# Linear attention with relu features on one core: four heads per 128 partitions for K and V, masked K, and nine output stores queued behind the loads

## The chip, the core and the metric

The kernel runs on one core of a Trainium2 chip. The metric is device time in microseconds (us). Before the change it is 131.75 us, the median of 10 runs that lie between 131.35 and 132.35 us.

## What is computed

The inputs Q, K and V and the output are float32 tensors of shape (8, 12, 512, 64): batch, heads, sequence, head dimension. Cut to what matters:

```python
Q_feat = np.maximum(0, Q)
K_feat = np.maximum(0, K)
KV = einsum('bhkd,bhkv->bhdv', K_feat, V)        # per head: 64 x 64
K_sum = sum(K_feat, axis=2)                      # per head: 64
numerator = einsum('bhqd,bhdv->bhqv', Q_feat, KV)
denominator = einsum('bhqd,bhd->bhq', Q_feat, K_sum)
out = numerator / (denominator[..., None] + 1e-10)
```

There are 96 heads in all, each independent of the others. A head's K, V, Q and output are 128 KB each in float32, so the core has to read 37.75 MB and write 12.58 MB.

## The kernel before

**Tiling.** The 96 heads are cut into 24 groups of four (NG = 24). One group's Q is a tile of 128 partitions by 1024 values: a head takes 32 partitions, and each partition holds 16 consecutive sequence rows of 64, which are 4 KB of consecutive DRAM in float32. The output has the same layout. K and V have another layout: two pairs of heads, and in each pair a head takes 64 partitions with 8 sequence rows each. A partition therefore reads two separate runs of 2 KB (`rview`, with j the pair).

**Loads.** All loads but the first K and V cast float32 to bfloat16 on the way and are issued from GpSimd (POOL): `load_kv` (L81 for K, L83 for V) and `load_q` (L87). They stand in one queue, q0 in the profile, in program order. Every DMA of that queue waits for the one eight places ahead of it, so at most eight are in flight. K and V of group 0 come in float32 over SP and ACT (L91, L93). K and V have 20 buffers each; Q has one for every group.

**Stores.** Group g's output leaves as 512 KB in float32 (`store`). Groups 0 to 16 and 22 leave over SP (L189, queue q1). Group 23 leaves over SP in two halves (L186). The five groups 17 to 21 (HELD = 5) leave over POOL (L182). All loads are issued ahead of them in POOL's program, so these stores stand behind every load in q0.

**Steps of one group.** The order is written out by hand in the last loop:

- `prep(g)` on VectorE (DVE): relu of K into bfloat16, written twice side by side (L114, 128x2048), and two copies of V into the halves of a block-diagonal tile `vbd` with a column of ones per head (L120, 64x1024 each). The zeros of `vbd` are written once for each of its three buffers (`zero`, L105 to L108).
- `mm_kv(g)` on TensorE (PE): for each of two pairs and eight rows r one matmul, 128 rows deep, 128 columns of K as weights and 130 columns of `vbd` moving (L128), 16 in all. Because `vbd` is block-diagonal, the two heads of a pair stay apart.
- `evac_kv(g)` on ScalarE (ACT): two copies of the sums from PSUM into a block-diagonal tile `kvd` (L137, 64x260).
- `transp(g)` on PE: eight 128x128 transposes of Q (L143), and `evac_qt(g)` on ACT: relu from PSUM to SBUF (L147).
- `mm_out(g)` on PE: 32 matmuls with 32 weight columns and 130 moving ones (L158), and `norm(g)` on DVE: denominator, reciprocal and product for two halves (L169, L171, L172), then the store.

The loop runs `mm_kv(g)`, `evac_kv(g)`, `prep(g+1)`, then `mm_out(g-1)` with `norm(g-1)` and its store, then `transp(g)` and `evac_qt(g)`. Each engine takes its instructions in that order. The sums of `mm_kv` have two PSUM buffers.

Of the kernel before, what the change touches and what calls it, by code (L numbers as in the profile page):

```python
# [9 lines left out]
@with_exitstack  # L10
def kernel(
    ctx: ExitStack,
    tc: tile.TileContext,
    Q: bass.AP,
    K: bass.AP,
    V: bass.AP,
    out: bass.AP,
):
    nc = tc.nc
    B, H, S, D = Q.shape  # L20
    assert D == 64
    P = 128
    D1 = D + 1
    NH = B * H


    R = S * 2 // P
    RQ = S * 4 // P
    PR = 2
    NHG = 2 * PR  # L30
    U = RQ // 2
    NG = NH // NHG
    assert NG * NHG == NH and R == 8 and RQ == 16
    HELD = 5

    fp32 = mybir.dt.float32
    bf16 = mybir.dt.bfloat16
    Act = mybir.ActivationFunctionType
    Alu = mybir.AluOpType

    def pool(name, bufs, **kw):
        return ctx.enter_context(tc.tile_pool(name=name, bufs=bufs, **kw))

    consts = pool("consts", 1)
    qin = pool("qin", NG)
    kin = pool("kin", 20)
    vin = pool("vin", 20)
    kfp = pool("kfp", 3)
    qtp = pool("qtp", 3)
    rcp = pool("rcp", 4)  # L50
    outp = pool("outp", 10)
    pkv = pool("pkv", 2, space=bass.MemoryType.PSUM)
    pqt = pool("pqt", 2, space=bass.MemoryType.PSUM)
    pou = pool("pou", 2, space=bass.MemoryType.PSUM)

    def rview(X):
        return X.rearrange("b h s d -> (b h s d)").rearrange(
            "(n j p f) -> n p j f", p=P, f=R * D, j=PR)

    def qview(X):  # L60
        return X.rearrange("b h s d -> (b h s d)").rearrange("(n p f) -> n p f", p=P, f=RQ * D)

    Qr, Kr, Vr, Or = qview(Q), rview(K), rview(V), qview(out)

    ident = consts.tile([P, P], bf16, name="ident")
    NB = 3

    vbf = [consts.tile([P, PR * R * 2 * D1], bf16, name=f"vbd{i}") for i in range(NB)]  # L70
    kvf = [consts.tile([P, PR * 2 * 2 * D1], bf16, name=f"kvd{i}") for i in range(NB)]
    vbd = [x.rearrange("p (j r h d) -> p j r h d", j=PR, r=R, h=2) for x in vbf]
    kvd = [x.rearrange("p (j h t d) -> p j h t d", j=PR, h=2, t=2) for x in kvf]

    ctx.enter_context(tc.manual_schedule())

    q_sb, k_sb, v_sb = {}, {}, {}

    def load_kv(g):
        k_sb[g] = kin.tile([P, PR, R, D], bf16, name="k_sb")  # L80
        nc.gpsimd.dma_start(out=k_sb[g].rearrange("p j r d -> p j (r d)"), in_=Kr[g])  # L81
        v_sb[g] = vin.tile([P, PR, R, D], bf16, name="v_sb")
        nc.gpsimd.dma_start(out=v_sb[g].rearrange("p j r d -> p j (r d)"), in_=Vr[g])  # L83

    def load_q(g):
        q_sb[g] = qin.tile([P, U, 2 * D], bf16, name="q_sb")
        nc.gpsimd.dma_start(out=q_sb[g].rearrange("p u f -> p (u f)"), in_=Qr[g])  # L87


    k_sb[0] = outp.tile([P, PR, R, D], fp32, name="k_first", tag="o_sb")  # L90
    nc.sync.dma_start(out=k_sb[0].rearrange("p j r d -> p j (r d)"), in_=Kr[0])  # L91
    v_sb[0] = outp.tile([P, PR, R, D], fp32, name="v_first", tag="o_sb")
    nc.scalar.dma_start(out=v_sb[0].rearrange("p j r d -> p j (r d)"), in_=Vr[0])  # L93
    load_q(0)
    make_identity(nc, ident)
    for g in range(1, NG - 2):
        load_kv(g)
        load_q(g)
    load_kv(NG - 2)
    load_kv(NG - 1)  # L100
    load_q(NG - 2)
    load_q(NG - 1)

    def zero(i):
        nc.vector.memset(vbf[i].bitcast(fp32), 0.0)  # L105
        for h in range(2):
            nc.vector.memset(vbd[i][64 * h:64 * h + 64, :, :, h, D:D1].rearrange("p j r o -> p (j r) o"), 1.0)
        nc.vector.memset(kvf[i].bitcast(fp32), 0.0)  # L108

    kf, qt, ps_kv, ps_qt, ps_out = {}, {}, {}, {}, {}  # L110

    def prep(g):
        kf[g] = kfp.tile([P, PR, R, 2, D], bf16, name="kf")
        nc.vector.tensor_scalar(  # L114
            kf[g].rearrange("p j r c d -> p (j r) c d"),
            k_sb[g].rearrange("p j r d -> p (j r) d").unsqueeze(2).to_broadcast([P, PR * R, 2, D]),
            scalar1=0.0, scalar2=None, op0=Alu.max)
        for h in range(2):
            hs = slice(64 * h, 64 * h + 64)
            nc.vector.tensor_copy(  # L120
                vbd[g % NB][hs, :, :, h, 0:D].rearrange("p j r d -> p (j r) d"),
                v_sb[g][hs].rearrange("p j r d -> p (j r) d"))

    def mm_kv(g):
        ps_kv[g] = pkv.tile([P, PR, 2, D1], fp32, name="ps_kv")
        for j in range(PR):
            for r in range(R):
                nc.tensor.matmul(  # L128
                    ps_kv[g][:, j, :, :],
                    kf[g][:, j, r, :, :].rearrange("p c d -> p (c d)"),  # L130
                    vbd[g % NB][:, j, r, :, :],
                    start=(r == 0), stop=(r == R - 1), skip_group_check=True)

    def evac_kv(g):
        for t in range(2):
            ts_ = slice(64 * t, 64 * t + 64)
            nc.scalar.copy(kvd[g % NB][ts_, :, :, t, :].rearrange("p j h d -> p (j h) d"),  # L137
                           ps_kv[g][ts_].rearrange("p j h d -> p (j h) d"))

    def transp(g):  # L140
        ps_qt[g] = pqt.tile([P, U, P], bf16, name="ps_qt")
        for u in range(U):
            nc.tensor.transpose(ps_qt[g][:, u, :], q_sb[g][:, u, :], ident)  # L143

    def evac_qt(g):
        qt[g] = qtp.tile([P, U, P], bf16, name="qt")
        nc.scalar.activation(  # L147
            qt[g].rearrange("p u q -> p (u q)"), ps_qt[g].rearrange("p u q -> p (u q)"), Act.Relu)

    def mm_out(g):  # L150
        for j in range(2):
            po = pou.tile([P, 2, 512], fp32, name="ps_out")
            ps_out[g, j] = po
            for v in range(U // 2):
                u = j * (U // 2) + v
                for h in range(NHG):
                    hs = slice(32 * h, 32 * h + 32)
                    nc.tensor.matmul(  # L158
                        po[hs, v // 2, (v % 2) * 2 * D1:(v % 2) * 2 * D1 + 2 * D1],
                        qt[g][:, u, hs],  # L160
                        kvd[g % NB][:, h // 2, h % 2, :, :],
                        start=True, stop=True, skip_group_check=True)

    def norm(g):
        o_sb = outp.tile([P, RQ, D], fp32, name="o_sb", tag="o_sb")
        for j in range(2):
            pv = ps_out[g, j][:, :, 0:4 * D1].rearrange("p b (r d) -> p b r d", d=D1)
            den = rcp.tile([P, 2, 4], fp32, name="den")
            nc.vector.tensor_scalar(den, pv[:, :, :, D], scalar1=1e-10, scalar2=None, op0=Alu.add)  # L169
            rec = rcp.tile([P, 2, 4], fp32, name="rec")  # L170
            nc.vector.reciprocal(rec, den)  # L171
            nc.vector.tensor_tensor(  # L172
                o_sb[:, 8 * j:8 * j + 8].rearrange("p (b r) d -> p b r d", b=2),
                pv[:, :, :, 0:D],
                rec.unsqueeze(3).to_broadcast([P, 2, 4, D]), op=Alu.mult)
        return o_sb

    def store(g, o_sb):  # L180
        if NG - 2 - HELD <= g < NG - 2:
            nc.gpsimd.dma_start(out=Or[g], in_=o_sb.rearrange("p r d -> p (r d)"))  # L182
        elif g == NG - 1:
            for j in range(2):
                rs = slice(RQ // 2 * j, RQ // 2 * (j + 1))
                nc.sync.dma_start(out=Or[g].rearrange("p (r d) -> p r d", d=D)[:, rs],  # L186
                                  in_=o_sb[:, rs])
        else:
            nc.sync.dma_start(out=Or[g], in_=o_sb.rearrange("p r d -> p (r d)"))  # L189

    zero(0)
    prep(0)
    for g in range(NG):
        mm_kv(g)
        evac_kv(g)
        if g + 1 < NG:
            if g + 1 < NB:
                zero(g + 1)
            prep(g + 1)
        if g > 0:  # L200
            mm_out(g - 1)
            store(g - 1, norm(g - 1))
        transp(g)
        evac_qt(g)
    mm_out(NG - 1)
    store(NG - 1, norm(NG - 1))


# [28 lines left out]
```

## Time and profile before

| what | value |
|---|---|
| median of 10 runs | 131.75 us (131.35 to 132.35) |
| the profiled execution's own time | 132.17 us |
| its span, first to last instruction | 130.4 us |
| PE busy | 78.0 us (60%), 1344 matmuls |
| weight loads (PEld) busy | 64.2 us (49%) |
| DVE busy | 90.2 us (69%) |
| ACT busy | 43.9 us (34%) |
| POOL busy | 51.9 us (40%) |
| granted TensorE clock, mean | 0.78 of full |
| DMA packets | 20126, 32.18 MB as written |
| read from and written to HBM | 37.75 MB and 12.58 MB, 386 GB/s over the span |

The span is the time from the first to the last instruction of the program; the profiled execution took 1.8 us more than its span. A casting load is counted by the bytes that it writes to SBUF, half of what it reads from DRAM: that is why the packets sum to 32.18 MB and the HBM traffic to 50.33 MB. The profile's "DMA share" is the summed time of all packets over that of 16 DMA engines, and it goes above 1 where packets overlap.

### The profile page before, as it was taken

To read this page: it belongs to the slowest core of one execution; us is meant where nothing else is said; L and a number is where in the kernel's file an instruction comes from. 1 tells how busy PE (TensorE), PEld (TensorE's weight loads), DVE (VectorE), ACT (ScalarE), POOL (GpSimd) and SP (SyncE) were. 2 spreads that over 40 slices of the span, in tenths; PEclk is the share of its full clock that TensorE was granted. 3 is DMA by queue.
4 is the path that set the end of the run, shared out by engine and by line. 5 is a ranking of instruction groups with operands and counts; after the bars stand their busy time and mean duration, and the time that the engine had idled before them with its cause. 6 is when DMAs were issued, how large, how long until landed. Compare 5 with 4: busy or idle time off the path is not lost.

```text
span 130.4 us, 3249 instructions
## 1 busy us (share of the span) xinstructions
PE 78.0 (60%) x1344; PEld 64.2 (49%) x1344; DVE 90.2 (69%) x228; ACT 43.9 (34%) x73; POOL 51.9 (40%) x81
## 2 busy tenths in 40 slices
PE   0067974294595495685765756658439429758620
PEld 0066853263483384474554655457338328546510
DVE  4488995468567568586685675775857759979860
ACT  1205555024324323433235235233432432533600
POOL 6985452234435326144344252342433436312100
PEclk9999999959559558658657756856995995995996
DMA  3999999999999999999999999999999999999982
GB/s 126 288 208 203 203 185 230 309 207 271 217 286 257 231 286 235 253 285 214 274 269 220 285 247 243 282 227 263 275 213 285 258 231 207 205 212 363 379 344 95
DMA packets 20126, 32.18 MB, mean 247 GB/s; under 512 B 1552, under 2 KB 13328, under 8 KB 20112
## 3 DMA queue, kind: packets, MB, share of 16 engines
q0 software_dynamic: 16688, 20.98, 87.3%
q1 hardware_dynamic: 3152, 10.49, 21.5%
q10 hardware_dynamic: 272, 0.52, 1.1%
q8 instruction: 10, 0.16, 0.5%
q14 instruction: 4, 0.03, 0.1%
HBM read 37.75 MB, written 12.58 MB: 386 GB/s over the span
## 4 chain that ended last, share of the span: by engine, by line
DMA 86%; PE 3%; issue 3%; POOL 2%; DVE 2%; ACT 1%; ACTq 0%; POOLq 0%
DMA q_sb<-in_Q_dram 38%; DMA k_sb<-in_K_dram 27%; DMA v_sb<-in_V_dram 21%; PE ps_kv L128 1%; PE ps_qt L143 1%; DVE o_sb L172 1%; PE ps_out L158 1%; ACT qt L147 1%; POOL v_sb L83 1%; POOL k_sb L81 1%; POOL q_sb L87 0%; DVE rec L171 0%; POOL ident masks.py:199 0%; DVE den L169 0%; POOL ident masks.py:197 0%
## 5 line engine op out<-in xcount | busy, mean ns | idle before, releaser
L128 PE MATMUL ps_kv<-vbd,kf 128*128 128x130 bf16 x384 | 35.7, 265 | 37.3 <-DVE vbd L120 37.2
L128 PEld LDWEIGHTS <-kf 128*128 128x128 bf16 x384 | 32.7, 121 | 40.1 <-issue 28.9
L147 ACT ACTIVATE qt<-ps_qt 128x1024 bf16<-128x1024 bf16 x24 | 24.6, 1025 | 31.6 <-PE ps_qt L143 31.6
L172 DVE TENSOR_TENSOR o_sb<-ps_out,rec 128x512 f32<-128x512 f32 x48 | 33.2, 691 | 1.7
L137 ACT CAST kvd<-ps_kv 64x260 bf16<-64x260 f32 x48 | 18.0, 375 | 45.5 <-PE ps_kv L128 44.9
L158 PE MATMUL ps_out<-kvd,qt 128*32 128x130 bf16 x768 | 23.5, 272 | 9.1 <-DVE o_sb L172 6.1
L120 DVE COPY vbd<-v_sb 64x1024 bf16<-64x1024 bf16 x46 | 19.8, 431 | 12.8 <-DMA v_sb<-in_V_dram 12.4
L87 POOL DMA_DIRECT2D q_sb<-in_Q_dram x24 | 14.4, 598 | 32.5 <-DMA k_sb<-in_K_dram 31.2
L114 DVE TENSOR_SCALAR kf<-k_sb 128x2048 bf16<-128x2048 bf16 x23 | 15.9, 691 | 14.0 <-DMA k_sb<-in_K_dram 13.9
L81 POOL DMA_DIRECT2D k_sb<-in_K_dram x23 | 16.8, 733 | 18.0 <-DMA v_sb<-in_V_dram 15.9
L158 PEld LDWEIGHTS <-qt 128*32 128x32 bf16 x768 | 15.4, 116 | 15.8 <-DVE o_sb L172 8.5
L143 PE MATMUL ps_qt<-ident,q_sb 128*128 128x128 bf16 x192 | 21.8, 283 | 0.1
L83 POOL DMA_DIRECT2D v_sb<-in_V_dram x23 | 17.1, 745 | 10.8 <-DMA q_sb<-in_Q_dram 9.3
L143 PEld LDWEIGHTS <-q_sb 128*128 128x128 bf16 x192 | 16.4, 129 | 4.2 <-issue 3.2
L171 DVE RECIPROCAL rec<-den 128x8 f32<-128x8 f32 x48 | 9.7, 203 | 1.6
L169 DVE TENSOR_SCALAR den<-ps_out 128x8 f32<-128x8 f32 x48 | 7.7, 160 | 1.2 <-PE ps_out L158 0.5
L182 POOL DMA_DIRECT2D out_dram<-o_sb x5 | 2.9, 579 | 9.0 <-DVE o_sb L172 5.1
L105 DVE MEMSET vbd<- 128x1040 f32 x3 | 2.8, 925 | 1.6 <-PEq L221 1.0
L114 DVE TENSOR_SCALAR kf<-k_first 128x2048 bf16<-128x2048 f32 x1 | 1.2, 1226 | 2.5 <-DMA k_first<-in_K_dram 2.5
L137 ACT ACT_TABLE_LOAD x1 | 1.3, 1283 | 2.8 <-DVE kvd L108 2.8
L120 DVE CAST vbd<-v_first 64x1024 bf16<-64x1024 f32 x2 | 1.4, 705 | 0.0
L108 DVE MEMSET kvd<- 128x260 f32 x3 | 0.8, 275 | 0.3
(7 smaller groups left out, 1.3 us busy)
## 6 DMA issues: line engine op xcount, KB each, us to landing
out_dram<-o_sb SPq DMA_DIRECT2D x18, 512.0 KB, 6.5
q_sb<-in_Q_dram POOLq DMA_DIRECT2D x24, 256.0 KB, 12.5
k_sb<-in_K_dram POOLq DMA_DIRECT2D x23, 256.0 KB, 14.0
v_sb<-in_V_dram POOLq DMA_DIRECT2D x23, 256.0 KB, 13.9
out_dram<-o_sb POOLq DMA_DIRECT2D x5, 512.0 KB, 8.9
v_first<-in_V_dram ACTq DMA_DIRECT2D x1, 512.0 KB, 4.9
k_first<-in_K_dram SPq DMA_DIRECT2D x1, 512.0 KB, 4.4
out_dram<-o_sb SPq DMA_DIRECT2D x2, 256.0 KB, 3.1
```

The source lines that it names most:

```text
L81: nc.gpsimd.dma_start(out=k_sb[g].rearrange("p j r d -> p j (r d)"), in_=Kr[g])
L83: nc.gpsimd.dma_start(out=v_sb[g].rearrange("p j r d -> p j (r d)"), in_=Vr[g])
L87: nc.gpsimd.dma_start(out=q_sb[g].rearrange("p u f -> p (u f)"), in_=Qr[g])
L114: nc.vector.tensor_scalar(kf[g].rearrange("p j r c d -> p (j r) c d"), k_sb[g].rearrange("p j r d -> p (j r) d").unsqueeze(2).to_broadcast ...
L120: nc.vector.tensor_copy(vbd[g % NB][hs, :, :, h, 0:D].rearrange("p j r d -> p (j r) d"), v_sb[g][hs].rearrange("p j r d -> p (j r) d"))
L128: nc.tensor.matmul(ps_kv[g][:, j, :, :], kf[g][:, j, r, :, :].rearrange("p c d -> p (c d)"), vbd[g % NB][:, j, r, :, :], start=(r == 0), s ...
L137: nc.scalar.copy(kvd[g % NB][ts_, :, :, t, :].rearrange("p j h d -> p (j h) d"), ps_kv[g][ts_].rearrange("p j h d -> p (j h) d"))
L143: nc.tensor.transpose(ps_qt[g][:, u, :], q_sb[g][:, u, :], ident)
L147: nc.scalar.activation(qt[g].rearrange("p u q -> p (u q)"), ps_qt[g].rearrange("p u q -> p (u q)"), Act.Relu)
L158: nc.tensor.matmul(po[hs, v // 2, (v % 2) * 2 * D1:(v % 2) * 2 * D1 + 2 * D1], qt[g][:, u, hs], kvd[g % NB][:, h // 2, h % 2, :, :], start ...
L171: nc.vector.reciprocal(rec, den)
L172: nc.vector.tensor_tensor(o_sb[:, 8 * j:8 * j + 8].rearrange("p (b r) d -> p b r d", b=2), pv[:, :, :, 0:D], rec.unsqueeze(3).to_broadcast ...
```

## The change

K and V take the layout of Q: four heads on 128 partitions, 16 sequence rows and 4 KB per partition. A head now has 32 partitions, and two heads share each 64-partition half. To keep these two apart, `prep` writes relu(K) twice, each time multiplied by a mask column that is 1 on every second head's partitions and 0 on the others'. V is no longer block-diagonal: one copy into a dense tile `vo` with 65 columns per row (64 and the one). `mm_kv` runs 32 matmuls of 64 rows' depth, two halves t alternating, each half into its own PSUM bank. The four heads' sums lie in a different order, and `evac_kv` takes four copies in place of two. The sums have one PSUM buffer of two banks in place of two buffers.

Around it: nine groups of stores (13 to 21) in place of five stand behind the loads in POOL's queue; K and V of the first two groups come in float32 over SP and ACT; the buffers for K, V and Q are 14 each, those for outputs 13 in place of 10.

```diff
-    R = S * 2 // P
-    RQ = S * 4 // P
-    PR = 2
-    NHG = 2 * PR
+    NHG = 4
+    R = S * NHG // P
...
-    HELD = 5
+    HELD = 9
+    F32 = 2
...
-    qin = pool("qin", NG)
-    kin = pool("kin", 20)
-    vin = pool("vin", 20)
+    qin = pool("qin", 14)
+    kin = pool("kin", 14)
+    vin = pool("vin", 14)
...
-    outp = pool("outp", 10)
-    pkv = pool("pkv", 2, space=bass.MemoryType.PSUM)
+    outp = pool("outp", HELD + 4)
+    pkv = pool("pkv", 1, space=bass.MemoryType.PSUM)
...
     def rview(X):
-        return X.rearrange("b h s d -> (b h s d)").rearrange(
-            "(n j p f) -> n p j f", p=P, f=R * D, j=PR)
+        return X.rearrange("b h s d -> (b h s d)").rearrange("(n p f) -> n p f", p=P, f=R * D)
...
-    k_sb[0] = outp.tile([P, PR, R, D], fp32, name="k_first", tag="o_sb")
-    nc.sync.dma_start(out=k_sb[0].rearrange("p j r d -> p j (r d)"), in_=Kr[0])
-    v_sb[0] = outp.tile([P, PR, R, D], fp32, name="v_first", tag="o_sb")
-    nc.scalar.dma_start(out=v_sb[0].rearrange("p j r d -> p j (r d)"), in_=Vr[0])
+    for g in range(F32):
+        k_sb[g] = outp.tile([P, R, D], fp32, name="k_first", tag="o_sb")
+        nc.sync.dma_start(out=k_sb[g].rearrange("p r d -> p (r d)"), in_=Kr[g])
+        v_sb[g] = outp.tile([P, R, D], fp32, name="v_first", tag="o_sb")
+        nc.scalar.dma_start(out=v_sb[g].rearrange("p r d -> p (r d)"), in_=Vr[g])
...
     def prep(g):
-        kf[g] = kfp.tile([P, PR, R, 2, D], bf16, name="kf")
-        nc.vector.tensor_scalar(
-            kf[g].rearrange("p j r c d -> p (j r) c d"),
-            k_sb[g].rearrange("p j r d -> p (j r) d").unsqueeze(2).to_broadcast([P, PR * R, 2, D]),
-            scalar1=0.0, scalar2=None, op0=Alu.max)
-        for h in range(2):
-            hs = slice(64 * h, 64 * h + 64)
-            nc.vector.tensor_copy(
-                vbd[g % NB][hs, :, :, h, 0:D].rearrange("p j r d -> p (j r) d"),
-                v_sb[g][hs].rearrange("p j r d -> p (j r) d"))
+        kf[g] = kfp.tile([P, R, 2, D], bf16, name="kf")
+        for s in range(2):
+            nc.vector.tensor_scalar(kf[g][:, :, s, :], k_sb[g], scalar1=0.0,
+                                    scalar2=mask[:, s:s + 1], op0=Alu.max, op1=Alu.mult)
+        nc.vector.tensor_copy(vo[g % NB][:, :, 0:D], v_sb[g])

     def mm_kv(g):
-        ps_kv[g] = pkv.tile([P, PR, 2, D1], fp32, name="ps_kv")
-        for j in range(PR):
-            for r in range(R):
+        ps_kv[g] = pkv.tile([P, 2, 512], fp32, name="ps_kv")
+        for r in range(R):
+            for t in range(2):
+                ts_ = slice(64 * t, 64 * t + 64)
                 nc.tensor.matmul(
-                    ps_kv[g][:, j, :, :],
-                    kf[g][:, j, r, :, :].rearrange("p c d -> p (c d)"),
-                    vbd[g % NB][:, j, r, :, :],
+                    ps_kv[g][:, t, 0:D1],
+                    kf[g][ts_, r, :, :].rearrange("p s d -> p (s d)"),
+                    vo[g % NB][ts_, r, :],
                     start=(r == 0), stop=(r == R - 1), skip_group_check=True)

     def evac_kv(g):
-        for t in range(2):
-            ts_ = slice(64 * t, 64 * t + 64)
-            nc.scalar.copy(kvd[g % NB][ts_, :, :, t, :].rearrange("p j h d -> p (j h) d"),
-                           ps_kv[g][ts_].rearrange("p j h d -> p (j h) d"))
+        for s in range(2):
+            for c in range(2):
+                nc.scalar.copy(kvd[g % NB][64 * c:64 * c + 64, :, s, c, :],
+                               ps_kv[g][64 * s:64 * s + 64, :, 0:D1])
```

`mm_out`, `transp`, `evac_qt`, `norm` and the hand-written order of the steps stay as they are. The loads of K and V are 44 in POOL's queue in place of 46, each of 128 rows of 4 KB in place of 256 rows of 2 KB.

## The prediction

> **What bounds the kernel now.** I read the page's slices and queues first, then the waits, then busy time by stretch, then the records of single DMA packets and landings.
>
> ```profile
> DMA  3999999999999999999999999999999999999982
> ...
> q0 software_dynamic: 16688, 20.98, 87.3%
> q1 hardware_dynamic: 3152, 10.49, 21.5%
> ```
>
> The DMA engines are full from the second slice to the last but two. POOL's queue q0 and SP's q1 add up to 108.8% of 16 engines: packets overlap, so a packet's own time isn't what it costs.
>
> ```profile
> POOL q_sb L87 <- DMA k_sb<-in_K_dram: 31.2, 19, 2.1
> ...
> DVE kf L114 <- DMA k_sb<-in_K_dram: 13.9, 16, 1.0
> DVE vbd L120 <- DMA v_sb<-in_V_dram: 12.4, 18, 3.0
> ```
>
> POOL waits for earlier loads before it may issue more, and DVE waits for K and V as they land (us, times, longest). Compute follows the loads.
>
> ```profile
> 8.00:16.00 8.00, 7.14 (x94) 6.58 (x93) 6.88 (x18) 3.24 (x6) 4.56 (x7) 1.00 1.20 205
> 50.00:70.00 20.00, 13.66 (x224) 11.22 (x223) 14.10 (x36) 6.79 (x12) 7.80 (x12) 0.66 1.16 257
> ...
> 108.00:116.00 8.00, 5.88 (x112) 4.78 (x111) 6.74 (x18) 3.55 (x6) 3.14 (x6) 0.81 1.22 206
> 118.00:124.00 6.00, 4.58 (x92) 3.90 (x96) 5.42 (x16) 2.80 (x4) 1.28 (x2) 0.73 0.99 378
> ```
>
> Columns: stretch, length, busy PE, PEld, DVE, ACT, POOL, granted clock, DMA share, GB/s. GB/s counts written bytes. Loads alone (8 to 16, 108 to 116) write 205, so read 410 from DRAM. A group in the middle writes 3 x 256 + 512 KB and moves 2048 KB in DRAM: 257 x 1.6 = 411. Stores alone reach 378. The bound is thus bytes, near 410 GB/s, nearly the same whether rows are 2 KB (two loads of three) or 4 KB. PE, at most 14.0 of 20 us, and DVE, 14.1, have room.
>
> ```profile
> 118.40 0.74 POOL L182 DMA_DIRECT2D out_dram<-o_sb  x1 [2.31 <-DVE o_sb L172]
> 121.95 0.53 POOL L182 DMA_DIRECT2D out_dram<-o_sb  x1 [2.81 <-DVE o_sb L172]
> ```
>
> In the tail POOL's last two held stores wait 2.3 and 2.8 us for their data (start, duration, in brackets the idle time before). By the landing records the typical engine then has gaps, but the slowest one lands every 1.24 us to the end, at 129.37 us: it is full. It runs 2.6 us behind the first at 117 us, 0.7 us at 12 us.
>
> [...]
>
> **The change, part by part.**
>
> *Rows of 4 KB.* A 2 KB packet took 98.8 ns, a 4 KB load packet 173.6: two against one save 24 ns, 12%, if packets were the bound. They overlap, so I price what landings show. While only loads run (6 to 19 and 107 to 118 us), the first engine finishes K or V 1.28 us after the DMA ahead, Q 1.257 us: 0.022 us. For 44 loads: 1.0 us. A least-squares fit of 1 us stretches (22 to 116 us) to the packet counts gives 80.5 ns per 2 KB packet, 157 per 4 KB load and 166 per store: 4 ns x 8 rows per engine x 44 = 1.4. I take **-1.2 us**, ends -0.8 and -1.6. The group that moves to SP and ACT has the same bytes; nothing.
>
> *Nine stores held.* Groups 13 to 16 move from beside the loads to behind them. Beside loads one costs 1.30 us (5.12 us a group at 257 GB/s, less three loads at 1.27) to 1.33 (8 x 166 ns); behind them, by landing, 1.25. Four save 0.2 to 0.3; the last held stores will also be ready, so the tail has no gap. As the slowest engine has none now, I give that 0.2 and not the 0.8 that the typical engine lost. **-0.5 us**, ends -0.2 and -1.1. On POOL four more issues of 0.54 us stand behind all loads and ahead of nothing. SP's remaining stores (22, 23) are issued while q0 still has some 11 us of stores, no longer after it: harmless.
>
> *Instructions.* 16 more matmuls and weight loads each per group are 768 instructions, three more 16 KB fetches. Bytes: 0.1 us. But a fetch sits on one engine: at 112.6 and 120.8 us the slowest one's landings came 1.92 and 1.81 us apart in place of 1.26. If all three hit it, 3 x 0.65 = 1.9; with ten such over the run it fell back some 2 us, so most don't. **+0.3 us**, ends 0 and 1.9.
>
> *Compute, priced at nothing*, as long as it keeps up. While SP stores run, a group of DMA is 5.1 us. From group 14 on, loads alone take 3 x 1.26 = 3.8 us, so compute must come near that:
>
> ```profile
> L128 PE MATMUL ps_kv<-vbd,kf 128*128 128x130 bf16 x384 | 35.7, 265 | 37.3 <-DVE vbd L120 37.2
> L172 DVE TENSOR_TENSOR o_sb<-ps_out,rec 128x512 f32<-128x512 f32 x48 | 33.2, 691 | 1.7
> L137 ACT CAST kvd<-ps_kv 64x260 bf16<-64x260 f32 x48 | 18.0, 375 | 45.5 <-PE ps_kv L128 44.9
> L120 DVE COPY vbd<-v_sb 64x1024 bf16<-64x1024 bf16 x46 | 19.8, 431 | 12.8 <-DMA v_sb<-in_V_dram 12.4
> L114 DVE TENSOR_SCALAR kf<-k_sb 128x2048 bf16<-128x2048 bf16 x23 | 15.9, 691 | 14.0 <-DMA k_sb<-in_K_dram 13.9
> ```
>
> DVE: norm is 2 x (691 + 203 + 160) = 2.11 us. Before, prep is 0.69 + 2 x 0.43 = 1.55, in all 3.66. After: two masked relus and one copy of 1024 elements, each like L120's 0.43: 1.29, in all **3.40**. L120 wrote half its rows at an odd column (65) and was no slower, so `vo`'s odd pitch should do. Upper bound if the masks lose the fast mode: L114 and L120 give 0.26 ns per element and 161 ns fixed; at a quarter rate 1.22 us each, 4.98 in all. Lower than 3.40 isn't possible, since the elements don't shrink.
>
> ACT: four copies of 130 elements for two of 260; each between half of 375 and 375 ns, so 0.75 to 1.50 for 0.75. With L147's 1.03 at most 2.5 us a group: hidden. In the last group up to +0.75, in an end no longer on the path.
>
> PE: `mm_kv` takes 1.89 us for 16 at half clock, 1.10 at full. For 32 with half the columns: as low as that, or with weight loads in the open as slow as a transpose (1.03 / 8 = 129 ns at half clock, 0.62 / 8 = 78 at full), 4.1 or 2.5. I take 2.2 at half clock[...]. With 1.06 and 1.03 for `mm_out` and transposes: 4.3 at half clock, some 2.5 at full; worst 6.2 and 3.8.
>
> *The single sum buffer* makes `mm_kv(g+1)` wait for `evac_kv(g)`. Queued behind it on PE are `mm_out(g)` and transposes, for which ACT and DVE wait. ACT's 0.75 to 1.5 us lie under `mm_out(g-1)` and `transp(g)`, 2.1 us at half clock, 1.3 at full. Without that cover, up to 1.5 us a group. The 14-buffer pools hold loads at most 14 groups ahead, and eight DMAs are 2.7 groups: no wait.
>
> **Slack.** Before, the load of Q 22 lands at 118.83 us and DVE ends at 126.47: a tail of 7.6 us. After, loads end earlier by four stores x 1.33 and 1.2, about 6.5 us, so DVE would end near 120. Behind the loads stand nine held stores and the last two, 11 x 1.25 = 13.8 us, until about 128. Compute may thus lag 4 to 5 us for nothing: its last store needs about 3 us more.
>
> **Sum:** -1.2 - 0.5 + 0.3 = -1.4 us on the profiled 132.17 (span 130.4, 1.8 around it). That execution was 0.4 above the median of 131.75, so the median becomes 130.35: **130.4 us**.
>
> **The rivals.**
>
> *A, my forecast* (0.50): the bound is bytes; 130.4, own range 129.4 to 131.2.
>
> *B, packets bound it after all* (0.13): 46 loads' worth x 8 x 24 ns = 8.8 us, / 1.16 overlap = 7.6 at most, 124; with the typical engine setting the tail, half of that, 128. For it: share over 1 and the gaps. Against: 410 GB/s in every mix.
>
> *C, PE falls behind* (0.14), the slower side: weight loads are not hidden in `mm_kv`. Place: groups 14 to 23. Between 6.2 and 3.8 us a group, at the granted 0.7 some 4.8; over 3.8 that is 1.0 x 9 = 9 us of lag, 4 to 5 above the slack: last DVE near 129, end near 134. It decides from about 4.3 us a group. For it: clock 0.66, PE already 0.69 busy. [...]
>
> *D, masks lose the fast mode* (0.06): DVE 24 x 4.98 + 5.2 start + some 7 of waits, 132 and the last store: about 135.
>
> *E, nothing moves* (0.17): fetches and the slow engine take back the gain: 131.3 to 132.0.
>
> **Numbers.** About 0.3% (0.4 us) is what this measurement can tell from no change. Faster: 0.47 of A, all of B, 0.04 of E: 0.64. Same: 0.03 of A and 0.08 of E: 0.11. Slower: C, D and 0.05 of E: 0.25. The range leaves out most of B below, half of C and D above: 128.3 to 133.0.
>
> **What would show it.** Right: SP's stores gone from about 87 us until group 22's, K, V and Q loads all landing 1.26 us apart, last load near 112 to 114 us, no wait of POOL for `o_sb` in the tail, DVE prep near 1.3 us. C: DVE or ACT waiting on `ps_kv`, PE over 90% busy late. D: masked relu at 1.2 us. B: loads alone reading clearly over 420 GB/s. I am wrong if the slowest engine's lag grows past 4 us, or if loads of 4 KB rows pace no better than 1.28 us.

## The result

The changed kernel takes **133.01 us** (median of 9 runs, 132.9 to 133.44), the kernel before 131.58 beside it (32 runs, 131.32 to 132.35). The ratio is 1.0109, interval [1.0094, 1.0123]: 1.1% slower, where 130.4 us was forecast.

The profiled execution of the changed kernel took 132.88 us, its span 131.1. The slices and queues of its page first:

```profile
span 131.1 us, 4110 instructions
...
DMA  3999999999999999999999999999999999999920
GB/s 117 382 288 209 210 184 279 275 244 261 253 242 283 247 249 284 232 264 273 231 279 260 231 286 254 240 210 210 211 209 211 210 212 237 397 412 420 397 98 0
...
q0 software_dynamic: 11088, 22.55, 82.1%
q1 hardware_dynamic: 2592, 8.91, 18.0%
```

Here the forecast seems to have come true. From 85 to 108 us loads alone write 209 to 212 GB/s (205 before), the stores behind them run at 397 to 420 (378 in 118 to 124 us before), and the DMA engines have no gap. But the last slice, 3.3 us long, is empty; before, it had a 2. The same in stretches (columns: stretch, length, busy PE, PEld, DVE, ACT, POOL, granted clock, DMA share, GB/s):

```profile
8.00:16.00 8.00, 5.88 (x157) 4.65 (x151) 5.56 (x15) 4.64 (x13) 3.15 (x5) 1.00 1.13 219
50.00:70.00 20.00, 12.77 (x284) 9.31 (x280) 12.66 (x36) 8.33 (x20) 6.30 (x12) 0.50 1.10 259
90.00:100.00 10.00, 7.51 (x190) 5.42 (x185) 8.22 (x24) 5.19 (x14) 4.04 (x8) 0.67 1.12 210
116.00:124.00 8.00, 1.06 (x32) 0.79 (x32) 2.71 (x7) 1.01 (x1) 0.00 (x0) 0.50 1.03 417
124.00:131.00 7.00, 0.00 (x0) 0.00 (x0) 0.00 (x0) 0.00 (x0) 0.00 (x0) 0.50 0.18 71
```

By the landing records the last load lands at 113.29 us (120.08 before) and the last output at **127.13 us, 2.24 us earlier than before** (129.37). As the traced execution of before was 0.4 us above its median and this one 0.1 below, some 1.7 of the 2.24 is the change's, by estimate. The page counts busy time of engines only, and after 124 us there is none. What fills the rest stands among the instructions of the launch line, which is where the program's end is written down. First the kernel before, then after (engine, operation, count; shortest, median and longest in ns; first and last start in us):

```profile
L232 SPq EVENT_SEMAPHORE  x12: 17/28/28, 126.9 to 130.3; - x12
L232 POOLq DRAIN  x3: 51/93/5476, 121.9 to 130.1; - x3
```

```profile
L227 SPq EVENT_SEMAPHORE  x12: 17/28/6726, 120.3 to 131.0; - x12
L227 POOLq DRAIN  x3: 51/102/15212, 115.1 to 130.8; - x3
```

The first DRAIN on POOL's sequencer begins as POOL issues its last store (121.95 us before, 115.13 after) and ends only after all of POOL's DMAs have landed. Before it ran 121.92 to 127.40, ended 0.46 us after POOL's last landing (126.94) and lay beside SP's last stores, which landed at 129.37. After it runs 115.11 to **130.32**, 3.19 us past POOL's last landing, at 127.13, which is now the last of all. The closing sequence of some 0.8 us follows, to 131.1. (SP's long wait, 6.7 us from 120.3, is for its own last store, which lands at 127.03.) From the last landing to the end of the span are 4.0 us in place of 1.0.

The chain of waits doesn't show this: it names DMA for 77% of the span and POOL's sequencer for 0%.

### The profile page after: what moved, and what is told of

Read it like the earlier page. It is cut to its first block, busy times and chain, and to the rows that moved or that the text cites. A ratio compares the mean times of both kernels' runs of the same rounds, so it can differ in the third digit from the quotient of the medians.

```text
span 131.1 us, 4110 instructions
## 1 busy us (share of the span) xinstructions
PE 72.7 (55%) x1728; PEld 54.1 (41%) x1728; DVE 80.2 (61%) x230; ACT 51.0 (39%) x121; POOL 44.3 (34%) x83
## 3 DMA queue, kind: packets, MB, share of 16 engines
q0 software_dynamic: 11088, 22.55, 82.1%
## 4 chain that ended last, share of the span: by engine, by line
DMA 77%; DVE 4%; PE 3%; POOL 3%; issue 2%; ACT 2%; ACTq 0%; POOLq 0%
DMA v_sb<-in_V_dram 29%; DMA q_sb<-in_Q_dram 27%; DMA k_sb<-in_K_dram 20%; DVE o_sb L167 2%; ACT qt L142 2%; PE ps_out L153 1%; PE ps_qt L138 1%; DVE vo L115 1%; PE ps_kv L123 1%; POOL q_sb L81 1%; POOL k_sb L75 1%; POOL v_sb L77 1%; DVE kf L113 1%; DVE rec L166 0%; DVE den L164 0%
## 5 line engine op out<-in xcount | busy, mean ns | idle before, releaser
L123 PE MATMUL ps_kv<-vo,kf 64*128 64x65 bf16 x768 | 23.6, 231 | 31.8 <-DVE vo L115 31.5
L132 ACT CAST kvd<-ps_kv 64x130 bf16<-64x130 f32 x96 | 25.3, 264 | 31.3 <-PE ps_kv L123 29.6
L123 PEld LDWEIGHTS <-kf 64*128 64x128 bf16 x768 | 20.1, 120 | 37.3 <-DVE vo L115 29.2
L153 PE MATMUL ps_out<-kvd,qt 128*32 128x130 bf16 x768 | 27.5, 292 | 11.6 <-DVE o_sb L167 6.7
L113 DVE TENSOR_SCALAR kf<-k_sb,mask 128x1024 bf16<-128x1024 bf16 x44 | 19.4, 483 | 18.6 <-DMA k_sb<-in_K_dram 18.6
L75 POOL DMA_DIRECT2D k_sb<-in_K_dram x22 | 12.0, 544 | 16.7 <-DMA v_sb<-in_V_dram 8.5
L77 POOL DMA_DIRECT2D v_sb<-in_V_dram x22 | 11.7, 531 | 16.0 <-DMA q_sb<-in_Q_dram 9.9
L115 DVE COPY vo<-v_sb 128x1024 bf16<-128x1024 bf16 x22 | 9.5, 431 | 9.6 <-DMA v_sb<-in_V_dram 9.6
L177 POOL DMA_DIRECT2D out_dram<-o_sb x9 | 4.9, 547 | 6.7 <-DVE den L164 1.6
L113 DVE TENSOR_SCALAR kf<-k_first,mask 128x1024 bf16<-128x1024 f32 x4 | 2.8, 749 | 5.3 <-DMA k_first<-in_K_dram 5.3
```

What stands on the lines that cost most here:

```text
L75: nc.gpsimd.dma_start(out=k_sb[g].rearrange("p r d -> p (r d)"), in_=Kr[g])
L77: nc.gpsimd.dma_start(out=v_sb[g].rearrange("p r d -> p (r d)"), in_=Vr[g])
L113: nc.vector.tensor_scalar(kf[g][:, :, s, :], k_sb[g], scalar1=0.0, scalar2=mask[:, s:s + 1], op0=Alu.max, op1=Alu.mult)
L115: nc.vector.tensor_copy(vo[g % NB][:, :, 0:D], v_sb[g])
L123: nc.tensor.matmul(ps_kv[g][:, t, 0:D1], kf[g][ts_, r, :, :].rearrange("p s d -> p (s d)"), vo[g % NB][ts_, r, :], start=(r == 0), stop=(r ...
L132: nc.scalar.copy(kvd[g % NB][64 * c:64 * c + 64, :, s, c, :], ps_kv[g][64 * s:64 * s + 64, :, 0:D1])
```

## The experiments

**Theory.** The drain takes time of its own after the last landing (3.19 us here), and it has come onto the path because POOL's stores are now last. **Rivals.** The 4 KB layout itself or the compute costs the time; or it is the nine stores in whatever queue. How long the drain takes, and from what, was open, and the first forms of the theory were wrong.

*The nine stores from SP.* SP is held by a tiny copy that reads the last V load; then it issues the nine. POOL has nothing left but loads.

```diff
     def store(g, o_sb):
+        if g == NG - 2 - HELD:
+            nc.sync.dma_start(out=gate, in_=v_sb[NG - 1][0:1, 0, :])
         if NG - 2 - HELD <= g < NG - 2:
-            nc.gpsimd.dma_start(out=Or[g], in_=o_sb.rearrange("p r d -> p (r d)"))
+            nc.sync.dma_start(out=Or[g], in_=o_sb.rearrange("p r d -> p (r d)"))
```

> The changed kernel with its nine held stores issued from SP in place of POOL; a tiny copy on SP that reads V of group 23 holds them until that load has landed. Theory (POOL's closing drain): in the changed kernel the last output lands at 127.1 us, but POOL's closing drain runs from 115.1 to 130.3 us, because its last store was issued 12 us before it landed. Without stores on POOL the drain ends with the loads, and the span ends about 1 us after the last landing: span 128 to 129, median 129.5 to 130.5, faster than before. Rival (the new layout's compute or its longer PE program costs the time): unchanged near 133.0.

Measured: 131.56 us (130.44 to 131.76, 21 runs), ratio 0.9978 [0.9965, 0.9992]; span 129.7. POOL's drain ends at 116.07, 2.82 us after POOL's last landing and hidden: that half held. The time missed the forecast, since the last landing is at 128.63. The stretches of this run show why:

```profile
108.00:112.00 4.00, 2.76 (x73) 1.99 (x71) 3.68 (x12) 2.05 (x5) 0.00 (x0) 0.71 0.88 163
112.00:116.00 4.00, 3.25 (x80) 2.56 (x80) 3.15 (x11) 2.07 (x6) 0.00 (x0) 0.72 0.93 352
116.00:124.00 8.00, 1.06 (x32) 0.79 (x32) 2.64 (x7) 0.92 (x1) 0.00 (x0) 0.50 1.02 406
```

The DMA share falls to 0.88 and 0.93: the gate opens so late that the loads run out before the first store is on its way. A later run opens the gate earlier.

*Five held, as before, in the new layout.*

```diff
-    HELD = 9
+    HELD = 5
...
-    outp = pool("outp", HELD + 4)
+    outp = pool("outp", 13)
```

> The changed kernel with five held stores on POOL as before (13 output buffers kept). Theory (drain): the last POOL store is issued later and lands earlier, so the drain ends before the last SP store has landed; span 128.5 to 129.5, median 130.2 to 131.2. Rival (layout): 132.5 to 133.5, since all of the new K, V and matmul layout is still there.

Measured: 130.68 us (6 runs), ratio 0.9927 [0.9908, 0.9947]; as expected. POOL's last landing comes at 125.40, its drain ends 3.02 us later, 128.42, only 0.45 past SP's last landing (127.97). So the layout isn't what costs time.

*Nine held in the old layout.*

```diff
-    HELD = 5
+    HELD = 9
...
-    kin = pool("kin", 20)
-    vin = pool("vin", 20)
+    kin = pool("kin", 14)
+    vin = pool("vin", 14)
...
-    outp = pool("outp", 10)
+    outp = pool("outp", 13)
```

> The kernel before with nine stores held on POOL (13 output buffers, 14 each for K and V). Theory (drain): the nine stores alone bring the loss into the old layout: last landing near 128.5 us but POOL's drain some 3 us later, span 131.5 to 132.5, median 133 to 134. Rival (layout): the held stores are harmless or a gain, 131.0 to 131.7.

Measured: 131.87 us (22 runs), ratio 1.0016 [1.0006, 1.0027]. **A miss**: POOL drains from 116.4 us, as early as in the changed kernel, and its last landing is at 128.18, near the end of all; yet the drain ends 0.62 us after it and not 3. Holding nine doesn't cost the time by itself either. Only both parts together do, and how early POOL's last DMA is issued isn't the reason.

*All the last stores on POOL*, groups 22 and 23 too, in the new layout.

```diff
         elif g == NG - 1:
             for j in range(2):
                 rs = slice(R // 2 * j, R // 2 * (j + 1))
-                nc.sync.dma_start(out=Or[g].rearrange("p (r d) -> p r d", d=D)[:, rs],
+                nc.gpsimd.dma_start(out=Or[g].rearrange("p (r d) -> p r d", d=D)[:, rs],
                                   in_=o_sb[:, rs])
+        elif g == NG - 2:
+            nc.gpsimd.dma_start(out=Or[g], in_=o_sb.rearrange("p r d -> p (r d)"))
```

> The changed kernel with the last two groups' stores on POOL too, behind the nine: POOL's last issue moves from 115 to about 120 us, with fewer DMAs in flight behind it. Theory, form 1 (the drain adds some 0.4 us per DMA that is in flight when it begins): last landing near 127.5, drain 1.5 to 2.5 us later, median 131.5 to 132.5. Form 2 (the drain ends at steps of some 4.9 us after the last issue): it ends 4.9, 9.8 us after 120.5, at 130.3, median near 133. Rival (drain harmless): span ends 1 us after the last landing wherever POOL issues, near 130.

Measured: 133.18 us (4 runs), ratio 1.0118 [1.0102, 1.0135]. The drain begins 5 us later, at 120.1, and ends 3.31 us after the last landing (127.19), slightly more than in the changed kernel. The number of POOL's DMAs still under way when the drain begins falls as a reason: with eight of them the changed kernel had 3.19 us and the old layout with nine held 0.62; with four, five held had 3.02 and the kernel before 0.46. A drain that looks up at fixed steps fits this run's end (130.50) but not the other runs at hand.

What did order the six traces was the count of everything that POOL had issued. Of the 11088 packets of q0 in the changed kernel 9856 carry data and 1232 have 4 bytes: 16 for each of POOL's 77 DMAs, as many as a DMA has landing records. A sixteenth of the page's count for q0, its mean over the 16 DMA engines, is 11088 / 16 = 693 in the changed kernel and 16688 / 16 = 1043 in the kernel before. The 3 us came in kernels with few packets, and there they grew with the number of DMAs, 68 in the first run, 80 in this one. The next runs ask which it is.

*2 KB rows in the changed kernel.* The SBUF tile gets a gap of 16 values in each row, so that a load is 256 packets of 2 KB again. All else stays (12 buffers in place of 14, to fit).

```diff
-        k_sb[g] = kin.tile([P, R, D], bf16, name="k_sb")
-        nc.gpsimd.dma_start(out=k_sb[g].rearrange("p r d -> p (r d)"), in_=Kr[g])
+        H2 = R // 2 * D
+        kt = kin.tile([P, 2, H2 + 16], bf16, name="k_sb")
+        nc.gpsimd.dma_start(out=kt[:, :, 0:H2], in_=Kr[g].rearrange("p (j f) -> p j f", j=2))
+        k_sb[g] = kt[:, :, 0:H2].rearrange("p j (r d) -> p j r d", d=D)
...
```

> The changed kernel with one thing put back: the SBUF tiles of K and V (groups 2 to 23) have a gap of 16 values in the middle of each partition's row, so that their loads again are 256 packets of 2 KB in place of 128 of 4 KB (12 buffers each in place of 14). So far POOL's closing drain ended 0.5 to 0.6 us after POOL's last landing in the two kernels with 2 KB packets and 2.8 to 3.3 us after it in the four with 4 KB packets. Theory (the drain's extra follows the packets of POOL's queue): it falls back to about 0.6 us; loads are slower by 1.0 to 1.4 us in all, so last landing near 128.4, span near 129.5, median near 131.3, faster than the changed kernel. Rival (the extra belongs to something else of the change): drain still 3 us after the landing, median 134 or more.

Measured: 131.81 us (13 runs), ratio 0.9998 [0.9988, 1.0009]. The launch line of this run:

```profile
L233 POOLq DRAIN  x3: 51/93/12462, 116.6 to 129.6; - x3
```

It waits as long as its DMAs run, then ends: 116.6 + 12.46 = 129.04, 0.46 us after POOL's last landing (128.58). Same order, same nine stores, same 77 DMAs, and the masked relu takes 483 ns in both: with more packets (and 12 buffers in place of 14) the 3.19 us became 0.46. They cost the DMA engines 1.6 us in exchange (last landing 128.73 against 127.13).

*The nine split*: groups 13 to 19 on POOL, 20 to 23 on SP.

```diff
-        if NG - 2 - HELD <= g < NG - 2:
+        if NG - 2 - HELD <= g < NG - 4:
```

> The changed kernel with seven groups held on POOL (13 to 19) and the next two (20, 21) stored from SP like 22 and 23, as soon as they are ready. Theory (drain): the DMA engines stay as full, last landing near 127.2, but POOL's last landing comes at 124.5 and its drain ends near 127.6; span near 128.3, median near 130.1. Rival (the end is set by something else than POOL's drain): 132 to 133.

Measured: 133.14 us (5 runs), ratio 1.009 [1.007, 1.011]. A miss. POOL's last landing doesn't come earlier: 127.47. With nine on POOL it was 127.13: SP's stores move beside POOL's and not behind them, and POOL's end as late as before. The drain ends 3.11 us after it, with 75 DMAs.

*Only one group in float32*, so two more DMAs on POOL.

```diff
-    F32 = 2
+    F32 = 1
...
```

> The changed kernel with only group 0's K and V in float32 over SP and ACT, as before. Both theories: no more than 0.3 us of difference from the changed kernel (132.7 to 133.3), and the drain's extra still near 3 us; if the extra falls to 0.5 us and the median to some 130.5, the way the first loads are issued is its cause.

Measured: 133.29 us (4 runs), ratio 1.0117 [1.0097, 1.0137]; drain 3.27 us past the last landing, with 79 DMAs.

*The gate opened earlier*: as in the first experiment, but SP's tiny copy reads V of group 22, which has four loads behind it.

```diff
+            nc.sync.dma_start(out=gate, in_=v_sb[NG - 2][0:1, 0, :])
```

> As the first experiment (nine stores held on SP, none on POOL), but the tiny copy that holds them reads V of group 22 in place of 23, so that they begin while some four loads are still queued: in the first experiment DMA throughput fell to 242 and 328 GB/s between 110 and 114 us, because the stores were let go too late. Theory (POOL's drain is the changed kernel's end, 41.4 ns for each of POOL's DMAs, and it is hidden when POOL ends early): no such hole, last landing 127.0 to 127.6, span 128.1 to 128.7, median 129.7 to 130.3, 1.0 to 1.5% faster than before. Rival (stores from SP cost more than from POOL): 131 or more.

Measured: **130.16 us** (130.01 to 130.25, 4 runs), ratio **0.9875 [0.9861, 0.9889]**. This beats both kernels. Stretches and launch line:

```profile
108.00:112.00 4.00, 3.04 (x71) 2.08 (x69) 3.56 (x11) 2.08 (x5) 0.00 (x0) 0.50 1.11 246
112.00:116.00 4.00, 3.63 (x80) 2.91 (x80) 2.81 (x8) 2.05 (x5) 0.00 (x0) 0.60 1.05 412
116.00:124.00 8.00, 0.64 (x32) 0.46 (x32) 3.09 (x10) 1.02 (x1) 0.00 (x0) 0.66 1.02 413
```

```profile
L230 POOLq DRAIN  x3: 51/93/12890, 103.8 to 128.1; - x3
```

The hole is gone, and the drain, 103.8 + 12.9 = 116.7 us, lies beside the stores. The last landing is at 127.39, as in the changed kernel (127.13), and the span ends 1.0 us later, at 128.4.

*The same gate and nine stores on SP in the old layout*, to have the layout's worth with the drain out of both.

```diff
-    HELD = 5
+    HELD = 9
...
+        if g == NG - 2 - HELD:
+            nc.sync.dma_start(out=gate, in_=v_sb[NG - 2][0:1, 0, 0, :])
```

> The kernel before with nine stores held on SP in the same way (hold on V of group 22). It takes POOL's drain out of both layouts. Theory: against it, the kernel of the run before this one shows what rows of 4 KB are worth by themselves, 1.0 to 1.4 us; so 130.9 to 131.5 here. Rival (the layout costs time by its matmuls, masks or instruction fetches): this one is the faster of the two.

Measured: 131.68 us (14 runs), ratio 0.9996 [0.9986, 1.0006], slightly above what was expected. Last landing 128.72. Against the run before, on the same chip: 131.68 - 130.16 = 1.5 us for the layout, with all that comes with it: the second group in float32 is in this figure and wasn't separated. The run gives one more point: 998 packets of q0 per engine (928 with data and 70 of 4 bytes), and the hidden drain ends 2.91 us after POOL's last landing. So short rows alone don't shorten the drain: all of its loads of K and V on POOL have rows of 2 KB.

*Some loads cut to 2 KB*, to count packets up to the edge: the first 34 of 44 loads of K and V have the gap (965 packets of q0 per engine, the "entries" of the two expectations), then the first 42 (1029). If the drain changes in a step between the runs with 712 and with 1043, 965 may still have the 3.2 us of the changed kernel (77 DMAs, 41.4 ns each); the 0.3 to 0.4 us expected for 1029 is an estimate of the author's that no trace had shown. A drain in proportion to the packets would take 1.1 us and 0.6.

```diff
+    CUT = 34
...
+        gap = 16 if 2 * (g - F32) < CUT else 0
```

> The changed kernel with 2 KB packets, as in the run with gaps, in the first 34 of POOL's 44 K and V loads only (the other ten without the gap). Per DMA engine POOL's DMAs then have 965 entries in all[...]. Theory [...] the drain ends 3.2 us after the last landing, median 133.6 to 134.2. Rival (the extra falls in proportion to the packets): 34 of 44 of the way from 3.19 to 0.46, 1.1 us, median near 132.

> The same with the first 42 of 44 loads: 1029 entries. Theory [...] the drain ends 0.3 to 0.4 us after the last landing, median near 131.7. If the limit lies between 1029 and 1043: 3.2 us and near 134. Rival (proportion): 0.6 us.

Measured: 134.25 us (2 runs), ratio 1.0186 [1.0164, 1.0208], and 131.56 us (18 runs), 0.9985 [0.9975, 0.9994]. Launch lines, with 34 cut and with 42:

```profile
L239 POOLq DRAIN  x3: 51/102/15347, 116.2 to 132.0; - x3
```

```profile
L239 POOLq DRAIN  x3: 51/102/10684, 118.2 to 129.6; - x3
```

POOL's last landings are at 128.34 and 128.51 us, so the drain ends 3.19 us after the one and 0.37 after the other. Eight loads more of 2 KB rows, which are slower to move (44 of them cost 1.6 us, above), make the kernel 2.7 us faster. It is a step between the two and not a proportion, and the number of buffers isn't it, as both runs have 12. (Counted in data packets alone it lies between 928 and 952 per engine.)

All thirteen traces together ("past" is the drain's end less POOL's last landing):

| kernel | packets of q0 per engine | POOL's DMAs | past, us | past / DMAs, ns |
|---|---|---|---|---|
| nine on SP, gate V 23 | 612 | 68 | 2.82 | 41.5 |
| nine on SP, gate V 22 | 612 | 68 | 2.82 | 41.5 |
| five held | 657 | 73 | 3.02 | 41.4 |
| split | 675 | 75 | 3.11 | 41.4 |
| **after** | 693 | 77 | 3.19 | 41.4 |
| one in float32 | 711 | 79 | 3.27 | 41.4 |
| all on POOL | 712 | 80 | 3.31 | 41.4 |
| 34 cut | 965 | 77 | 3.19 | 41.4 |
| old layout, nine on SP | 998 | 70 | 2.91 | 41.5 |
| 42 cut | 1029 | 77 | 0.37 | |
| **before** | 1043 | 75 | 0.46 | |
| 2 KB rows | 1045 | 77 | 0.46 | |
| old layout, nine held | 1079 | 79 | 0.62 | |

Up to 998 packets per engine the drain takes, past the last landing, 41.4 to 41.5 ns for each DMA that POOL issued in the whole program. From 1029 on it takes 0.4 to 0.6 us, more with more packets: 0.37 at 1029, 0.62 at 1079. Why there is a step between 998 and 1029, and why the time goes by POOL's DMAs below it, was not shown: the traces have the drain's start and end and nothing of its inside.

## Why the prediction was wrong

**The step that failed is in the sum: the time from the last landing to the end.** The prediction added up what moves the last landing and took the rest of the time as fixed. Of the four further stores on POOL it said that they stand "ahead of nothing", and of SP's last stores, which now come no longer after POOL's, that this is "harmless". POOL's stores stand ahead of POOL's closing drain. That drain was in the trace of before, in the launch line: it ended 2 us ahead of the last landing because SP's stores came last, and it was short, 0.46 us. The change took away both. It put POOL's landing last, and by halving the packets of 44 loads it brought the packets of q0 per engine from 1043 to 693. That fewer packets make the drain longer could not be read from the trace of before. That the drain lay hidden behind SP's stores could, and moving POOL's stores to the end of the span should have raised the question. No rival covered it: the slower ones put the lag in the compute.

The size: with POOL's drain behind other work the kernel has a ratio of 0.9875, with it in the open 1.0109. The difference is 2.3% or 3.1 us. In the traces 4.0 us pass from the last landing to the end of the span with the drain in the open and 1.0 with it hidden, a difference of 3.0.

**The rest of the sum held.** The forecast was -1.4 us. The run with the nine stores on SP, which differs from the change in little but the drain, has 130.16 against 131.75: -1.6. That the sum came this near doesn't show that its terms were right. The two large ones depend on each other, and how they split depends on the order in which they are taken:

- *Rows of 4 KB, -1.2 and +0.3 for fetches*: the layout is worth 131.68 - 130.16 = 1.5 us with nine held on SP in both. With five held on POOL in both it is 1.0 (ratio 0.9927), or 1.2 without the 0.2 us of drain that show there (next point). K and V loads land 1.25 to 1.26 us apart in place of 1.28. The page has 13 instruction fetches in q8 (0.21 MB) where that of before has 10 (0.16 MB), three more, as counted; in the 1.5 they are already paid.
- *Nine held, -0.5*: it depends on the layout. In the old layout nine in place of five gave +0.16% on POOL and -0.04% on SP: nothing, or slightly worse. The stores do land 1.25 us apart behind the loads, and POOL waits no more than 0.9 us for `o_sb`; a likely reason for the lack of gain, not tested, is that the slowest DMA engine was full in the tail anyway, with a landing every 1.24 us in the trace of before. In the new layout the step from five on POOL (0.9927) to nine on SP (0.9875) is 0.5%, 0.7 us. Some 0.2 of it is the drain that the five left in the open (1.24 us from the last landing to the end in place of 1.02), which leaves the 0.5 that was priced.
- *Compute, nothing*: right. The groups of the changed kernel (busy us, mean ns; idle before, and its cause):

```profile
L123 PE MATMUL ps_kv<-vo,kf 64*128 64x65 bf16 x768 | 23.6, 231 | 31.8 <-DVE vo L115 31.5
L132 ACT CAST kvd<-ps_kv 64x130 bf16<-64x130 f32 x96 | 25.3, 264 | 31.3 <-PE ps_kv L123 29.6
L113 DVE TENSOR_SCALAR kf<-k_sb,mask 128x1024 bf16<-128x1024 bf16 x44 | 19.4, 483 | 18.6 <-DMA k_sb<-in_K_dram 18.6
L115 DVE COPY vo<-v_sb 128x1024 bf16<-128x1024 bf16 x22 | 9.5, 431 | 9.6 <-DMA v_sb<-in_V_dram 9.6
```

The masked relu takes 483 ns where 430 was priced and 1.22 us for rival D, which is out. (A quarter of the rate is in the page of before, in L172: 691 ns for 512 float32 values, as long as L114 took for 2048 in bfloat16.) DVE's norm and prep come to 2.11 + 2 x 0.483 + 0.431 = 3.5 us a group (3.40 priced), and its last instruction ends at 119.9 us, near the 120 of the slack. ACT's four copies take 4 x 264 = 1.06 us, inside the 0.75 to 1.5. PE, from the stretch 50 to 70 us with four groups in it (20 ACT instructions, five a group): 12.77 / 4 = 3.2 us a group at half clock, where 4.3 was priced. `mm_kv`, priced at 2.2 by an estimate of the author's, as no matmul of before is 64 rows deep, took 1.06 us there (1.89 before, at half clock too):

```profile
59.75 1.06 PE L123 MATMUL ps_kv<-vo,kf 64*128 64x65 bf16 x32 [1.44 <-DVE vo L115]
```

So rival C is far off. DVE, the engine that could fall behind, waits for loads:

```profile
DVE kf L113 <- DMA k_sb<-in_K_dram: 18.6, 15, 1.7
...
DVE vo L115 <- DMA v_sb<-in_V_dram: 9.6, 19, 1.4
```

Rival B (packets as the bound) is out too: loads alone read 2 x 210 = 420 GB/s, at the edge of what the prediction set for it, and with the drain hidden the time is 130.16 us, not the 124 or 128 that it gave. Rival E (fetches and the slow engine take back the gain) didn't occur, as the last landing came forward. But one sign of being wrong that the prediction named did come: the slowest engine fell more than 4 us behind the first. In the changed kernel it landed the last store but one of POOL at 125.41 us, 4.76 us after the first engine (120.64). This isn't where the time went: with the nine on SP the lag stayed below 3.3 us, and the last landing was no earlier (127.39 against 127.13).

**What stays open**: what the drain does inside; whether 41.4 ns and the step between 998 and 1029 packets hold for DMAs of other shapes, as all here have 128 rows or 256; and why the runs of the first gate fell into two groups, 19 of 21 at 131.35 to 131.76 and two near 130.45.

## What to carry to other kernels

Ask of every change near the end which engine's DMAs land last, and what that engine's queue still does after them; the engines' closing instructions stand in the launch line of the trace, while busy shares and the chain of waits left them out here. Where loads go by POOL, as here, let POOL's last DMA land some 3 us ahead of the end (the drain's length here), and put the last stores on SP, held back by a tiny copy that reads a load which still has a few others behind it (here four: 130.16 us, against 131.56 with the last load of V). A gain in the transfers and a change of queue are to be summed apart: here the first was -1.6 us and the second about +3.

## What the runs showed that was not expected

- POOL's closing drain takes 41.4 to 41.5 ns per DMA of the whole program after POOL's last landing (2.82 us for 68, 3.31 for 80) up to 998 packets of q0 per DMA engine, and 0.4 to 0.6 us from 1029 on.
- So more packets made a kernel faster here: with 1029 per engine it took 131.56 us, with 965 134.25.
- Handing part of POOL's stores to SP didn't bring POOL's last landing forward while both had stores left: 127.47 with seven on POOL, 127.13 with nine.
- 32 matmuls of 64 rows' depth and 65 columns, two row tiles alternating, took 1.06 us at half clock, where 16 of 128 rows and 130 columns took 1.89. From 50 to 70 us PE was busy for 12.77 us against 13.66 before, though the granted clock was 0.50 against 0.66.
